# Down projection of a gated MLP on one core: products of 512 columns written as two of 256, except in the first and last block of inner rows

## The chip, the cores and the metric

The kernel runs on one core of one Trainium2 chip. The metric is the device time of one execution in microseconds; the time before is the median of three runs.

## What is computed

One layer of a hybrid decoder on 256 tokens of 1,024 features, in float32: a mixer (a matrix-memory branch and an attention branch, gated, summed, projected), a layer norm, and a gated MLP with a layer norm. The change lies in the MLP, cut here to what matters:

```python
def conv_gated_mlp(x, w_up, conv_ffn, w_down):
    u = causal_dwconv(jnp.einsum("bsd,df->bsf", x, w_up), conv_ffn)
    g, up = jnp.split(u, 2, axis=-1)
    return jnp.einsum("bsf,fd->bsd", jax.nn.silu(g) * up, w_down)

x = layer_norm(ALPHA * x + conv_gated_mlp(x, ...), ln2_g, ln2_b)
```

The inner width `D_FF` is 2,816, that is 22 blocks of 128 inner rows. The down projection multiplies 256 tokens x 2,816 inner rows by 2,816 x 1,024.

## The kernel before

**Weights as a stream.** All large weights come from HBM as steps of 128 x 2,048 floats (`load`, L80, issued on SP into three `raw` buffers). `chunk_order` (L45) writes out the order of the steps. The MLP's part of it is four `up` steps, then eight times a `dn` step followed by two `up` steps, then two more `up` steps and the last three `dn` steps. One `up` step holds one block of 128 inner rows (both halves of the gate); one `dn` step holds two blocks of inner rows with all 1,024 output columns. There are 22 `up` and 11 `dn` steps, numbered d = 0 to 10.

**Three products for one.** TensorE multiplies in a float32 form of less precision, so each operand is split into a high and a low part (`split_into`, L89: ACT writes the high part at L91, DVE the low part at L92), and `mm3` (L122) issues three products into the same accumulator: high x high at L125, then two mixed ones at L126 and L127. Each of them names a stationary operand of 128 x 128, which TensorE loads, and a moving operand, whose columns stream through.

**The up steps.** `mm_feat` (L129) takes the weights as stationary operand and the 256 tokens of `x1h`, `x1l` as moving one: 2 column blocks x 8 k-blocks x 3 = 48 products of 256 columns, into `ps_up`. ACT and DVE then apply the convolution taps and the gate (`up_evac`, L1004), and leave `hh` and `hl` (128 inner rows x 256 tokens) for a later `dn` step.

**The down steps.** `step_dn` (L1035) has the roles the other way round: `hh` or `hl` (128 tokens) is stationary, and the weight's columns move. The accumulators (`ffn` in the profile, L1038 to L1041) stay in PSUM for the whole projection. For the first 128 tokens (t = 0) they are two of 512 columns; for the second (t = 1) one of 512 and two of 256. So a block of inner rows k takes, in this order, 2 x 3 products of 512 columns for t = 0, then 3 of 512 and 2 x 3 of 256 for t = 1: nine of 512 and six of 256. Steps d = 0 to 7 (k = 0 to 15) do both halves of the tokens block by block. The last three steps (k = 16 to 21) are reordered: all six blocks for t = 0 (L1064), then all six for the 512-column accumulator of t = 1, then all six for each of its 256-column ones (L1070), so that the layer norm of the first half of the tokens (`part`, `ln_scale`, `ln2_out`) runs on DVE meanwhile.

The weight tiles `wh`, `wl` are shared by all steps; `shift` (L61) sets at which column of them a kind of step begins: 0 for the output projection `wo` and for `dn`, 16 for `up` and most of the input projection's steps, 48 or 56 for others. Accumulators named `mix` belong to `wo` steps, `ps_ga`, `ps_qb`, `ps_km`, `ps_kb`, `ps_vm` to steps of the input projection; all of these products have 256 columns. The products at L159 (`mm_early`, accumulators `ps_o`) have 512.

The instructions of each engine stand in the order in which the code issues them; there is no scheduler.

Of the kernel before, what the change touches and what calls it, by code (L numbers as in the profile page):

```python
# [24 lines left out]
NF = D_FF // P  # L25
# [44 lines left out]
class Kernel:  # L70
# [964 lines left out]
    def step_dn(self, s, d, *a):  # L1035
        if d == 0:
            self.st = [self.ln_tiles(f"2_{t}") for t in range(2)]
            a0 = [self.ps_side([P, 512], f"ffn0{h}") for h in range(2)]  # L1038
            a1 = [self.ps_side([P, 512], "ffn10"), self.ps_side([P, 256], "ffn11"), self.ps_side([P, 256], "ffn12")]
            self.acc = [list(zip(a0, ((0, 512), (512, 1024)))),  # L1040
                        list(zip(a1, ((0, 512), (512, 768), (768, 1024))))]  # L1041

        def mm(dd, kk, t, ps, cols):
            w = [x.rearrange("p (k f) -> p k f", k=2)[:, kk, slice(*cols)] for x in self.w[s - d + dd]]
            k = 2 * dd + kk
            hh, hl = (x[:, t * P:(t + 1) * P] for x in self.hid[k])
            self.mm3(ps, hh, hl, w[0], w[1], k == 0, k == NF - 1)

        def part(t, q):
            ps, cols = self.acc[t][q]  # L1050
            self.ln_part(self.st[t], self.x1[:, t, :], ps, cols)

        d0 = NF // 2 - 3
        if d < d0:
            for kk in range(2):
                for t in range(2):
                    for ps, cols in self.acc[t]:
                        mm(d, kk, t, ps, cols)
            self.w.pop(s)
            return  # L1060

        ks = [(d0 + i, kk) for i in range(3) for kk in range(2)]
        banks = self.acc[1]
        if d == d0:  # L1064
            for k in ks:
                for q in self.acc[0]:
                    mm(*k, 0, *q)
            self.evac[s] = [lambda: part(0, 0), lambda: part(0, 1), lambda: self.ln_scale(self.st[0]),
                            lambda: self.ln2_out(0)]
        else:  # L1070
            for q in banks[0:1] if d == d0 + 1 else banks[1:]:
                for k in ks:
                    mm(*k, 1, *q)
            if d == d0 + 1:
                self.evac[s] = [lambda: part(1, 0)]
# [111 lines left out]
```

## Time and profile before

| | |
|---|---|
| median of 3 runs | 497.76 us (497.49 to 497.85) |
| the profiled execution | 497.06 us |
| its span, first to last instruction | 495.3 us |
| mean granted TensorE clock | 0.995 |
| DVE, ACT busy | 370.3 us (75%), 287.9 us (58%) |
| DMA | 93.74 MB, mean 189 GB/s |

The span is 1.76 us shorter than the execution's own time; what lies around it is launch and end. In a row of the timeline stand the start in us, the duration in us, engine, line, operation, output<-inputs, the stationary and moving shape, and the count. The duration of a product (0.28 us for 256 columns) includes its way through the pipeline, and its end is modelled; products follow each other much faster than that. How fast they run is therefore read from their starts: the length of a stretch divided by the number of products that begin in it. In a row of the windows view stand the stretch (us from the span's start), its length, busy us and count of the instructions that touch it, the granted clock, the DMA engines' share and GB/s.

### The profile page before, as it was taken

What the parts mean: (1) busy time and instruction counts of PE and PEld (TensorE: products, weight loads), DVE (VectorE), ACT (ScalarE), POOL (GpSimd) and SP (SyncE); (2) the same over time, 40 slices, a digit from 0 to 9 for tenths busy, and PEclk for the clock granted to TensorE, in tenths of its full rate; (3) what the DMA queues carried; (4) which work ended last, traced back from release to release, by engine and by line L of the source; (5) the groups of instructions that cost most, each with busy time, mean ns of one, the idle gap of its engine ahead of it and who ended that gap; (6) DMA issues with size and microseconds to landing.
All of it is one profiled execution on the core that took longest, in us unless ns stands there. A gap on an engine that the chain in (4) does not pass through costs nothing.

```text
span 495.3 us, 9451 instructions
## 1 busy us (share of the span) xinstructions
PE 482.9 (97%) x3890; PEld 467.0 (94%) x3890; DVE 370.3 (75%) x659; ACT 287.9 (58%) x476; POOL 31.3 (6%) x46
## 2 busy tenths in 40 slices
PE   7999999999999999999999999999999999999992
PEld 3999999999999999999999999999999999999982
DVE  3966995788588858885677788888667766866886
ACT  4757867495648665866655524766554555554610
POOL 0600010002100110002000001000000000000001
PEclk9999999999999999999999999999999999999998
DMA  8984556456545654454945572745555456444202
GB/s 246 356 304 152 211 192 203 171 177 191 189 179 177 192 180 189 171 171 138 372 173 181 221 278 86 255 146 210 206 205 177 164 184 242 170 171 171 86 1 85
DMA packets 17884, 93.74 MB, mean 189 GB/s; under 512 B 4497, under 2 KB 4889, under 8 KB 7857
## 3 DMA queue, kind: packets, MB, share of 16 engines
q1 hardware_dynamic: 13682, 87.08, 49.4%
q0 software_dynamic: 4160, 6.07, 4.1%
q8 instruction: 30, 0.49, 0.4%
q14 instruction: 12, 0.10, 0.1%
HBM read 92.05 MB, written 2.63 MB: 191 GB/s over the span
## 4 chain that ended last, share of the span: by engine, by line
PE 96%; DMA 1%; DVE 1%; SPq 0%; ACT 0%; POOL 0%; issue 0%; POOLq 0%
PE ps_up L127 8%; PE ps_up L126 8%; PE ps_up L125 8%; PE ffn L127 4%; PE ffn L126 4%; PE ffn L125 4%; PE ps_vm L125 2%; PE ps_qm L125 2%; PE ps_vm L126 2%; PE ps_vm L127 2%; PE ps_vb L125 1%; PE ps_ga L127 1%; PE ps_ga L125 1%; PE ps_ga L126 1%; PE ps_vb L126 1%; PE ps_vb L127 1%
## 5 line engine op out<-in xcount | busy, mean ns | idle before, releaser
L92 DVE TENSOR_TENSOR wl<-raw,wh 128x1024 fp32r<-128x1024 f32 (+1 forms) x162 | 188.6, 1206 | 27.4 <-ACT wh L91 27.2
L91 ACT CAST wh<-raw 128x1024 fp32r<-128x1024 f32 (+1 forms) x162 | 158.4, 1030 | 10.7 <-DMA raw<-in_wst_dram 8.0
L127 PE MATMUL ps_up<-x1h,wl 128*128 128x256 f32 x320 | 89.9, 281 | 0.0
L126 PE MATMUL ps_up<-x1l,wh 128*128 128x256 f32 x320 | 89.9, 281 | 0.0
L125 PE MATMUL ps_up<-x1h,wh 128*128 128x256 f32 x319 | 89.7, 281 | 0.0
L126 PEld LDWEIGHTS ps_up<-x1l,wh 128*128 128x128 f32 x320 | 61.4, 192 | 0.0
L127 PEld LDWEIGHTS ps_up<-x1h,wl 128*128 128x128 f32 x320 | 60.1, 188 | 0.0
L125 PEld LDWEIGHTS ps_up<-x1h,wh 128*128 128x128 f32 x319 | 59.9, 188 | 0.0
L1020 DVE SCALAR_TENSOR_TENSOR cu<-ps_up,vec,cu 128x255 f32<-128x255 f32 (+1 forms) x80 | 33.1, 476 | 27.1 <-ACT cu L1016 26.9
L127 PE MATMUL ffn<-wh,hl 128*128 128x512 f32 (+1 forms) x110 | 38.4, 349 | 0.0
L126 PE MATMUL ffn<-wl,hh 128*128 128x512 f32 (+1 forms) x110 | 38.4, 349 | 0.0
L125 PE MATMUL ffn<-wh,hh 128*128 128x512 f32 (+1 forms) x110 | 38.3, 349 | 0.0
L91 ACT CAST hh<-cu 128x256 fp32r<-128x256 f32 x22 | 8.9, 407 | 42.9 <-DVE cu L1028 42.9
L1016 ACT ACTIVATE cu<-ps_up,vec 128x256 f32<-128x256 f32 x40 | 16.8, 472 | 28.8 <-PE ps_up L127 27.9
L126 PEld LDWEIGHTS ffn<-wl,hh 128*128 128x128 f32 x110 | 20.8, 189 | 3.0
L125 PEld LDWEIGHTS ffn<-wh,hh 128*128 128x128 f32 x110 | 20.7, 188 | 3.0
L127 PEld LDWEIGHTS ffn<-wh,hl 128*128 128x128 f32 x110 | 20.7, 188 | 2.9
L927 POOL TENSOR_TENSOR rs<-rs,mhalf 128x1 f32<-128x1 f32 x4 | 2.7, 666 | 247.6 <-DVE rs L926 247.6
L125 PE MATMUL ps_gb<-xth,wh 128*128 128x256 f32 x64 | 18.0, 282 | 0.0
L126 PE MATMUL ps_vm<-wl,xth 128*128 128x256 f32 x64 | 17.9, 280 | 0.0
L127 PE MATMUL ps_vm<-wh,xtl 128*128 128x256 f32 x64 | 17.9, 280 | 0.0
L125 PE MATMUL mix<-wh,mgh 128*128 128x256 f32 x64 | 17.8, 279 | 0.0
(295 smaller groups left out, 1442.8 us busy)
## 6 DMA issues: line engine op xcount, KB each, us to landing
raw<-in_wst_dram SPq DMA_DIRECT2D x78, 1024.0 KB, 4.9
raw<-in_wst_dram SPq DMA_DIRECT2D x5, 512.0 KB, 9.1
lnrow<-in_rows_dram POOLq DMA_DIRECT2D x4, 512.0 KB, 6.8
band<-table POOLq DMA_DIRECT2D x4, 384.0 KB, 12.3
toe<-band POOLq DMA_DIRECT2D x4, 256.0 KB, 4.4
xtok<-in_x_dram POOLq DMA_DIRECT2D x1, 1024.0 KB, 7.7
out_dram<-r SPq DMA_DIRECT2D x3, 256.0 KB, 2.0
raw<-in_wst_dram SPq DMA_DIRECT2D x2, 256.0 KB, 5.9
```

Of the source, the lines that this page charges most:

```text
L91: self.nc.scalar.copy(wh, raw)
L92: self.nc.vector.tensor_sub(wl, raw, wh.bitcast(F32))
L125: mm(ps, ah if first is None else first, bh, start=start, stop=False)
L126: mm(ps, ah, bl, start=False, stop=False)
L127: mm(ps, al, bh, start=False, stop=stop)
L927: nc.gpsimd.tensor_tensor(st["rs"], st["rs"], self.mhalf[:, 0:1], op=ALU.pow)
L1016: act.activation(cu[:, j, :], ps[:, j, :], AF.Copy, scale=tap(2, j))
L1020: v.scalar_tensor_tensor(cu[:, j, o:], ps[:, j, :S - o], tap(t, j), cu[:, j, o:], op0=ALU.mult, op1=ALU.add)
```

## The change

In `step_dn` the helper `mm` cuts a range of 512 columns into two of 256, unless the block of inner rows is the first (k = 0) or the last (k = 21). The two halves go into the two halves of the same accumulator, each with its own three products. Which parts of the operands are multiplied, and into which column of which accumulator, is unchanged; so are all other steps, all tiles and their addresses.

```diff
         def mm(dd, kk, t, ps, cols):
-            w = [x.rearrange("p (k f) -> p k f", k=2)[:, kk, slice(*cols)] for x in self.w[s - d + dd]]
             k = 2 * dd + kk
             hh, hl = (x[:, t * P:(t + 1) * P] for x in self.hid[k])
-            self.mm3(ps, hh, hl, w[0], w[1], k == 0, k == NF - 1)
+            n = cols[1] - cols[0] if k in (0, NF - 1) else 256
+            for c in range(cols[0], cols[1], n):
+                w = [x.rearrange("p (k f) -> p k f", k=2)[:, kk, c:c + n] for x in self.w[s - d + dd]]
+                o = c - cols[0]
+                self.mm3(ps[:, o:o + n], hh, hl, w[0], w[1], k == 0, k == NF - 1)
```

Here `cols` is the range of output columns of one accumulator and `ps` the accumulator. Of the 330 products of the projection before, 198 have 512 columns. 180 of them become 360 of 256; 18 stay (nine for k = 0, nine for k = 21). The program has 510 products in their place.

On PE, in the first down step (d = 0), the last product of k = 0 and the first ones of k = 1 stood like this before; `ffn_4072` and `ffn_4073` are the two accumulators of t = 0, `ffn_4076` the last of t = 1, `hh_3980` and `hl_3981` the inner rows of k = 1:

```order
L127 MATMUL ffn_4076<-wh_3878,hl_3971 128x256
L125 MATMUL ffn_4072<-wh_3878,hh_3980 128x512
L126 MATMUL ffn_4072<-wl_3879,hh_3980 128x512
L127 MATMUL ffn_4072<-wh_3878,hl_3981 128x512
L125 MATMUL ffn_4073<-wh_3878,hh_3980 128x512
```

In the changed program the same place on PE reads:

```order
L127 MATMUL ffn_4076<-wh_3878,hl_3971 128x256
L125 MATMUL ffn_4072<-wh_3878,hh_3980 128x256
L126 MATMUL ffn_4072<-wl_3879,hh_3980 128x256
L127 MATMUL ffn_4072<-wh_3878,hl_3981 128x256
L125 MATMUL ffn_4072<-wh_3878,hh_3980 128x256
L126 MATMUL ffn_4072<-wl_3879,hh_3980 128x256
L127 MATMUL ffn_4072<-wh_3878,hl_3981 128x256
L125 MATMUL ffn_4073<-wh_3878,hh_3980 128x256
```

The first three rows into `ffn_4072` are now its columns 0 to 255, the next three its columns 256 to 511. Between the 256-column products that end k = 0 and the `up` step that follows there is no product of 512 columns any more.

At the end of the projection, on PE in the changed program, the last block (k = 21, `hh_5768`) still has products of 512 columns, between pairs for t = 0 and pairs for t = 1 (`ffn_4074`):

```order
L127 MATMUL ffn_4073<-wh_5755,hl_5701 128x256
L125 MATMUL ffn_4072<-wh_5755,hh_5768 128x512
L126 MATMUL ffn_4072<-wl_5756,hh_5768 128x512
L127 MATMUL ffn_4072<-wh_5755,hl_5769 128x512
L125 MATMUL ffn_4073<-wh_5755,hh_5768 128x512
L126 MATMUL ffn_4073<-wl_5756,hh_5768 128x512
L127 MATMUL ffn_4073<-wh_5755,hl_5769 128x512
L125 MATMUL ffn_4074<-wh_5619,hh_5366 128x256
```

Of this piece only the first and last row were 512 columns wide before. DVE, ACT, POOL and SP have as many rows as before.

## The prediction

> **What bounds the kernel now.** I began with the page: TensorE (PE) is busy all the time, and the chain that ended last is almost wholly its own products, those of the up steps (`ps_up`) and of the down steps (`ffn`) ahead of all others.
>
> ```profile
> PE 482.9 (97%) x3890; PEld 467.0 (94%) x3890; DVE 370.3 (75%) x659; ACT 287.9 (58%) x476; POOL 31.3 (6%) x46
> ...
> PE 96%; DMA 1%; DVE 1%; SPq 0%; ACT 0%; POOL 0%; issue 0%; POOLq 0%
> PE ps_up L127 8%; PE ps_up L126 8%; PE ps_up L125 8%; PE ffn L127 4%; PE ffn L126 4%; PE ffn L125 4%; PE ps_vm L125 2%; PE ps_qm L125 2%; PE ps_vm L126 2%; PE ps_vm L127 2%; PE ps_vb L125 1%; PE ps_ga L127 1%; PE ps_ga L125 1%; PE ps_ga L126 1%; PE ps_vb L126 1%; PE ps_vb L127 1%
> ```
>
> The list of PE's waits has two entries, both from the first microseconds, so in the MLP nothing but PE's own pace sets the end:
>
> ```profile
> PE ps_o L159 <- ACT wh L91: 2.1, 2, 1.5
> PE warm_ps L194 <- DVE warm L191: 1.2, 1, 1.2
> ```
>
> So the question is at which pace products of 512 and of 256 columns follow each other. These rows are stretches without a break, from the windows view; the length divided by the products that begin in the stretch is the pace.
>
> ```profile
> 12.36:19.16 6.80, 6.80 (x31) 1.00 1.02 393
> ...
> 469.29:481.88 12.59, 12.59 (x54) 1.00 0.00 1
> ...
> 275.74:294.66 18.92, 18.92 (x167) 1.00 0.70 268
> ...
> 446.68:469.29 22.61, 22.61 (x192) 1.00 0.41 141
> ...
> 69.17:74.83 5.66, 5.66 (x48) 1.00 0.60 211
> 119.25:124.72 5.47, 5.46 (x48) 1.00 0.67 205
> ```
>
> First, 512 columns: the products at L159 take 6.80 / 30 = 226.7 ns (one of the 31 began earlier), those of the last down steps 12.59 / 54 = 233.1 ns. Then 256 columns: the output projection (`mix`, whose weights move as in the down steps) takes 18.92 / 167 = 113.3 ns, the last up steps 22.61 / 192 = 117.8 ns. The last two rows are the same step, `ps_ga`, in two groups of heads: 117.9 ns in the first, 114.0 ns in the second. The granted clock is 1.00 in all of them. So there are two paces for the same work, a quick one (113.3 ns per 256 columns, 226.7 per 512) and a slow one (117.8 and 233.1), and code and tile do not decide between them.
>
> What does is seen where the timeline passes from up to down steps and back (d = 0; k = 0 begins at 322.89, k = 1 at 325.67, the up steps at 328.47):
>
> ```profile
> 322.66 0.28 PE L126 MATMUL ps_up<-x1l,wh 128*128 128x256 f32 x1
> 322.78 0.28 PE L127 MATMUL ps_up<-x1h,wl 128*128 128x256 f32 x1
> 322.89 0.39 PE L125 MATMUL ffn<-wh,hh 128*128 128x512 f32 x1
> ...
> 324.99 0.28 PE L125 MATMUL ffn<-wh,hh 128*128 128x256 f32 x1
> 325.11 0.28 PE L126 MATMUL ffn<-wl,hh 128*128 128x256 f32 x1
> ...
> 325.67 0.39 PE L125 MATMUL ffn<-wh,hh 128*128 128x512 f32 x1
> 325.90 0.40 PE L126 MATMUL ffn<-wl,hh 128*128 128x512 f32 x1
> 326.14 0.39 PE L127 MATMUL ffn<-wh,hl 128*128 128x512 f32 x1
> 326.37 0.40 PE L125 MATMUL ffn<-wh,hh 128*128 128x512 f32 x1
> ...
> 327.77 0.28 PE L125 MATMUL ffn<-wh,hh 128*128 128x256 f32 x1
> ...
> 328.47 0.28 PE L125 MATMUL ps_up<-x1h,wh 128*128 128x256 f32 x1
> ...
> 339.78 0.39 PE L125 MATMUL ffn<-wh,hh 128*128 128x512 f32 x1
> ```
>
> The up steps come in slow. After the nine 512-column products of k = 0 the 256-column ones are quick (325.11 to 325.67, five steps in 0.56 us). After the nine of k = 1 they are slow again (327.77 to 328.47, six in 0.70 us: 117 ns), and the 96 products of the next two up steps stay slow: 11.31 us / 96 = 117.8 ns. So a pace is kept from product to product through a stretch of equal ones, and the 512-column products change it: nine that begin slow end quick, nine that begin quick end slow. In the timeline every down step to d = 7 repeats this.
>
> **The change part by part.** In the stretch from 325.67, where k = 1 begins, to 481.88, where the last 512-column product ends, I count the work in units of 256 columns: 18 up steps x 48 = 864; k = 1 to 15, each 9 x 2 + 6 = 24, 360; t = 0 of k = 16 to 21, 6 x 12 = 72; the 512-column accumulator of t = 1, 6 x 6 = 36. In all 1,332 units, and they took 156.21 us:
>
> ```profile
> 325.67:481.88 156.21, 156.21 (x1145) 1.00 0.47 169
> ...
> 325.67:481.88 156.21, 103.07 (x864) 1.00 0.47 169
> ```
>
> (The second row is `ps_up` alone; its 864 products confirm the count.)
>
> *Removed and added.* 180 products of 512 columns go, 360 of 256 come, 180 more weight loads with them. At the quick pace a pair takes 226.6 ns, as much as one quick product of 512 (226.7), so the extra loads cost nothing there. At the slow pace a pair takes 235.6 against 233.1, 2.5 ns more. Which applies depends on the pace when k = 1 begins. Up to 325.67 the program is unchanged, so it is quick.
>
> *What the removal changes behind it.* From 325.67 on, no 512-column product stands in the stream until k = 21. If the quick pace is kept, the up steps run at it too. I take it as kept, because equal streams keep theirs: 167 products in `mix`, and through step changes in the four steps from `ps_qb` on:
>
> ```profile
> 137.89:154.21 16.32, 16.32 (x147) 1.00 0.56 195
> 154.21:159.86 5.65, 5.65 (x50) 1.00 0.52 186
> ```
>
> The first row is `ps_qb`, `ps_km`, `ps_kb` (144 products begin in it, 113.3 ns each). The second is `ps_vm` (48 begin: 117.7 ns): there the quick pace was lost without any 512-column product. That is the evidence against me. In `ps_vm` the roles of weights and tokens swap, as they do from a down to an up step; but there the operands' start addresses change too (moving from 64 to 0 bytes past a multiple of 256, stationary from 128 to 64), while down steps, up steps and `mix` all have 64 and 128 by the program's addresses.
>
> *The sum.* 1,332 units x 113.3 ns = 150.92 us. At k = 21 the kept 512-column products leave and re-enter the quick pace: six from a quick start, then three, at 226 to 236 ns where quick ones take 226.7; that is about 9 x 5 ns = 0.05 us. 156.21 - 150.92 - 0.05 = 5.24 us saved; I say 5.2. By parts: the up steps 864 x (117.8 - 113.3) = 3.9; the pairs 180 x (233.1 - 226.6) = 1.2; the rest is 256-column products of odd k. The last 36 products (two accumulators of t = 1) stay slow: three 512-column products precede them, an odd number as with nine.
>
> *What else could hide the gain.* One round of down and two up steps lasts 16.9 us and would last 16.3. DVE, the busiest helper, has 11.72 us of work in it:
>
> ```profile
> 373.50:390.40 16.90, 16.90 (x128) 16.10 (x128) 11.72 (x18) 8.91 (x15) 0.00 (x0) 1.00 0.52 188
> ```
>
> That leaves over 4 us, and DMA is at 0.52; PE should wait for neither. At the end DVE waits for PE before its last sum:
>
> ```profile
> 486.32 0.42 DVE L919 SCALAR_TENSOR_TENSOR r<-x,ffn 128x256 f32<-128x256 f32 x1 [0.55 <-PE ffn L127]
> ```
>
> The products of t = 1 that end the stream shorten by only 15 pairs x 6.5 ns = 0.10 us, less than these 0.55, so the tail simply moves forward. The profiled execution would go from 497.06 (span 495.3) to 491.9 us; it stood 0.70 below the median, so the median goes from 497.76 to 492.5.
>
> **The rivals.** *The quick pace is lost at the first up step* (role swap, as at `ps_vm`), and nothing brings it back, since the 512-column products that did are gone. Then all is slow from 328.47 on: k = 1 takes 24 units x 113.3 ns, the rest 1,290 x 117.8 and nine 512-column products 9 x 233.1, together 156.78 us against 156.21, 0.6 us slower: 498.3. This is the case on the other side; it decides at one instruction, the first up product after k = 1. For it speaks `ps_vm`; against it, that the slow pace crosses the same border unharmed (327.77 to 339.78 above) and that `mix` follows differently addressed steps quickly. Chance 0.14. A measurement of this kernel can tell about 0.2% (1.0 us) from no change, so this would mostly show as the same: 0.10 for that, 0.04 for its exceeding 1.0 us.
>
> *Lost in every up step and found again in every down step*, because it belongs to the operands' roles after all. Then only the down steps' 468 units gain: 864 x 117.8 + 468 x 113.3 + 0.05 = 154.85 us, 1.4 saved: 496.4. For it: all up steps with these tiles are slow before. Against it: they are only ever seen behind slow products. Chance 0.05.
>
> *Each product has a cost of its own, and the paces are noise around it.* The slow rows give its size, 2.5 ns more for a pair: 180 x 2.5 = 0.45 us slower, 498.2. Against it stand the equal quick paces of one 512-column product and of a pair (226.7 and 226.6). Chance 0.03, all of it within 0.2%. By the Trainium skill (TensorE: Matmul & The Clock Gate, section Back-to-back issue gap) an isolated product costs its columns at 2.4 GHz plus about 2.5 ns, whatever its width; by that rule, which speaks against the change, 180 more products come to the same estimate, 0.45 us.
>
> **How the numbers follow.** The forecast case has 0.78 and its own range is 491.7 to 493.1: runs before spread by 0.36 us, and the quick pace may be off by 0.3 ns on 1,332 units, 0.4 us. To leave out no more than 2 in 10 the range must take in the case of 496.4 as well: 491.7 to 496.6. Faster by over 0.2%: 0.78 + 0.05 = 0.83; same 0.10 + 0.03 = 0.13; slower 0.04.
>
> **What would show it.** The windows view should give 5.44 us for a stretch of 48 `ps_up` products, not 5.65, and their mean duration should fall by the same 4 to 5 ns. The next `ffn` product after k = 1's up steps should start about 0.5 us earlier relative to 328.47. If `ps_up` stays at 117.8 and the `ffn` pairs take 235.6, the first rival is right; quick pairs beside slow up steps are the second. New waits in PE's list, or a DVE or DMA row as their releaser, would mean that the spare time was misjudged.

## The result, and the profile after

| | before | changed |
|---|---|---|
| median (4 runs each on one chip) | 497.69 us (497.49 to 497.85) | 490.5 us (490.16 to 491.2) |
| the profiled execution, and its span | 497.06, 495.3 us | 490.16, 488.4 us |
| first `ffn` product begins | 322.89 us | 321.25 us |
| first to last `ffn` product | 163.12 us | 157.92 us |
| last `ffn` product to the end of the span | 9.32 us | 9.28 us |

The changed kernel is faster: its ratio to the kernel before is 0.986, 95% interval 0.9849 to 0.9872. That is 7.2 us, 2.0 us more than the forecast and 1.2 us below its range. The last three rows of the table say where the time of the two profiled executions went: 5.20 us inside the projection, 0.04 us behind it, and 1.64 us ahead of it, where no instruction was changed. With 0.02 us less around the span they make the 6.90 us between the profiled executions. The medians lie 7.19 us apart, because before stood 0.63 us under its median in its profile and the changed kernel 0.34 us.

On the page TensorE is still the bound, with 180 more products, and its chain is the same:

```profile
PE 477.0 (98%) x4070; PEld 470.0 (96%) x4070; DVE 369.3 (76%) x659; ACT 286.2 (59%) x476; POOL 30.6 (6%) x46
...
PE 97%; DMA 1%; DVE 1%; SPq 0%; ACT 0%; issue 0%; POOL 0%; POOLq 0%
...
L127 PE MATMUL ps_up<-x1h,wl 128*128 128x256 f32 x320 | 88.5, 277 | 0.0
```

The last row is a group of up products, which the diff doesn't touch; its mean (the second number behind the bar) was 281 ns before. (The mean is of durations; the pace is read from starts, as before.) The windows view of `ps_up` in the changed kernel gives the stretch from k = 1 to the end of the last 512-column product, then the two up steps after k = 1, then the last four:

```profile
324.03:475.04 151.01, 99.22 (x864) 1.00 0.50 175
326.75:337.63 10.88, 10.88 (x96) 1.00 0.53 194
440.99:462.74 21.75, 21.75 (x192) 1.00 0.42 146
```

The stretch lasts 151.01 us where it lasted 156.21. Both groups of up steps run at 113.3 ns per product (10.88 / 96 and 21.75 / 192). In the timeline of the changed kernel one sees that the pace passes the border from down to up steps unchanged, and that the end is paced as before:

```profile
324.03 0.28 PE L125 MATMUL ffn<-wh,hh 128*128 128x256 f32 x1
...
326.64 0.28 PE L127 MATMUL ffn<-wh,hl 128*128 128x256 f32 x1
326.75 0.28 PE L125 MATMUL ps_up<-x1h,wh 128*128 128x256 f32 x1
...
343.07 0.28 PE L125 MATMUL ps_up<-x1h,wh 128*128 128x256 f32 x1
...
469.55 0.39 PE L125 MATMUL ffn<-wh,hh 128*128 128x512 f32 x1
...
470.95 0.28 PE L125 MATMUL ffn<-wh,hh 128*128 128x256 f32 x1
...
474.35 0.39 PE L125 MATMUL ffn<-wh,hh 128*128 128x512 f32 x1
...
475.05 0.28 PE L125 MATMUL ffn<-wh,hh 128*128 128x256 f32 x1
...
479.17 0.28 PE L127 MATMUL ffn<-wh,hl 128*128 128x256 f32 x1
...
479.49 0.42 DVE L919 SCALAR_TENSOR_TENSOR r<-x,ffn 128x256 f32<-128x256 f32 x1 [0.44 <-PE ffn L127]
```

The 24 products of k = 1 take 324.03 to 326.75, 113.3 ns each. One round of a down and two up steps is 326.75 to 343.07, 16.32 us. The last 36 products, behind the kept block k = 21, are slow: 35 steps from 475.05 to 479.17, 117.7 ns each.

The same rows show more than that a block of wide products (of 512 columns) turns the pace over. The nine products of k = 21 were 512 columns wide before and still are (of the piece shown ahead of the prediction for k = 21, only the first and the last row have changed their width): six for t = 0 (469.55 to 470.95), then three for t = 1 (474.35 to 475.05). Between the two groups stand 30 products of 256 columns, and they are quick (470.95 to 474.35, 113.3 ns each). So six wide products left the quick pace as it was, and three turned it over, as nine do at k = 0. All 20 profiles of this case agree: in their projections each of the 207 groups of nine wide products in a row and each of the four of three changed the pace; each of the four groups of six and of the 15 of 54 kept it. It is the odd number that counts.

The list of PE's waits in the changed kernel is as short as before, but one entry is 0.9 us smaller:

```profile
PE warm_ps L194 <- DVE warm L191: 1.2, 1, 1.2
PE ps_o L159 <- ACT wh L91: 1.2, 1, 1.2
```

This second row points to where the 1.64 us come from. Here are the first microseconds of the kernel before (the cast of the first weights on ACT, the first product that needs them, and the first of the next weight step):

```profile
6.49 0.62 ACT L91 CAST wh<-raw 128x512 fp32r<-128x512 f32 x1 [2.91 <-DMA raw<-in_wst_dram]
7.16 0.50 PE L159 MATMUL ps_o<-wh,xth 128*128 128x512 f32 x1 [1.47 <-ACT wh L91]
9.49 0.49 PE L159 MATMUL ps_o<-wh,xth 128*128 128x512 f32 x1 [0.66 <-ACT wh L91]
```

and the same three of the changed kernel:

```profile
3.98 0.62 ACT L91 CAST wh<-raw 128x512 fp32r<-128x512 f32 x1 [0.40 <-DMA raw<-in_wst_dram]
4.84 0.59 PE L159 MATMUL ps_o<-wh,xth 128*128 128x512 f32 x1
7.77 0.50 PE L159 MATMUL ps_o<-wh,xth 128*128 128x512 f32 x1 [1.19 <-ACT wh L91]
```

The first weights land 2.5 us earlier (here and below, "first weights" is the start of ACT's first cast of a weight). Some of that is spent waiting for the next step, whose first product comes 1.72 us earlier. From there PE has no further wait, and 1.64 us of it reaches the projection. The transfers are the same ones, issued on SP by the same instructions, those up to 3.11 us at the same times to 0.01 us; what differs is how fast they move. In the windows view (last column GB/s), the fifth microsecond of the kernel before:

```profile
4.00:5.00 1.00, 1.00 (x3) 0.30 (x2) 0.04 (x1) 0.00 (x0) 0.00 (x0) 1.00 0.66 92
```

and of the changed kernel:

```profile
4.00:5.00 1.00, 1.00 (x5) 0.44 (x3) 0.41 (x2) 0.60 (x1) 0.00 (x0) 1.00 0.90 251
```

The DMA view of the stretch from 2 to 6 us (packets, MB, share of the 16 engines) shows it more clearly, before and then changed:

```profile
q1 hardware_dynamic: 320, 0.54, 90.5%
```

```profile
q1 hardware_dynamic: 513, 0.99, 92.4%
```

The engines are busy in both, but a packet takes 181 ns before (90.5% of 16 x 4 us, divided by 320) and 115 ns in the changed kernel. So in the late beginning the transfers are not held back; each packet is slower.

So two theories were to be tested. On the projection: a pace is kept by history and turned over by a block of wide products (the prediction's), against "each pair of narrow products brings its own share". On the beginning: the longer program of TensorE does it, against chance between executions, buffers at other places, and the projection itself.

### The profile page after: what moved, and what is told of

The parts are those of the page before. It is cut to its first block, busy times and chain, and to the rows that moved or that the text cites. A ratio compares the mean times of both kernels' runs of the same rounds, so it can differ in the third digit from the quotient of the medians.

```text
span 488.4 us, 9811 instructions
## 1 busy us (share of the span) xinstructions
PE 477.0 (98%) x4070; PEld 470.0 (96%) x4070; DVE 369.3 (76%) x659; ACT 286.2 (59%) x476; POOL 30.6 (6%) x46
## 4 chain that ended last, share of the span: by engine, by line
PE 97%; DMA 1%; DVE 1%; SPq 0%; ACT 0%; issue 0%; POOL 0%; POOLq 0%
PE ps_up L127 8%; PE ps_up L125 8%; PE ps_up L126 8%; PE ffn L127 4%; PE ffn L126 4%; PE ffn L125 4%; PE ps_vm L125 2%; PE ps_qm L125 2%; PE ps_vm L126 2%; PE ps_vm L127 2%; PE ps_ga L125 2%; PE ps_ga L127 2%; PE ps_vb L125 2%; PE ps_vb L126 2%; PE ps_vb L127 2%; PE ps_ga L126 2%
## 5 line engine op out<-in xcount | busy, mean ns | idle before, releaser
L127 PE MATMUL ps_up<-x1h,wl 128*128 128x256 f32 x320 | 88.5, 277 | 0.0
L126 PE MATMUL ps_up<-x1l,wh 128*128 128x256 f32 x320 | 88.5, 276 | 0.0
L125 PE MATMUL ps_up<-x1h,wh 128*128 128x256 f32 x319 | 88.3, 277 | 0.0
L126 PEld LDWEIGHTS ps_up<-x1l,wh 128*128 128x128 f32 x320 | 60.2, 188 | 0.0
L127 PEld LDWEIGHTS ps_up<-x1h,wl 128*128 128x128 f32 x320 | 60.1, 188 | 0.0
L127 PE MATMUL ffn<-wh,hl 128*128 128x256 f32 (+1 forms) x170 | 47.7, 281 | 0.0
L126 PE MATMUL ffn<-wl,hh 128*128 128x256 f32 (+1 forms) x170 | 47.7, 281 | 0.0
L125 PE MATMUL ffn<-wh,hh 128*128 128x256 f32 (+1 forms) x170 | 47.7, 281 | 0.0
L126 PEld LDWEIGHTS ffn<-wl,hh 128*128 128x128 f32 x170 | 32.0, 188 | 0.3
L125 PEld LDWEIGHTS ffn<-wh,hh 128*128 128x128 f32 x170 | 31.9, 188 | 0.3
L127 PEld LDWEIGHTS ffn<-wh,hl 128*128 128x128 f32 x170 | 31.9, 188 | 0.3
L127 PE MATMUL ps_vm<-wh,xtl 128*128 128x256 f32 x64 | 17.9, 280 | 0.0
```

The source lines that it names most:

```text
L125: mm(ps, ah if first is None else first, bh, start=start, stop=False)
L126: mm(ps, ah, bl, start=False, stop=False)
L127: mm(ps, al, bh, start=False, stop=stop)
```

## The experiments on the pace

**The kernel before once more.** First, whether the early beginning is a matter of chance between two builds. No edit.

> The kernel before once more, for its first microseconds. Between the two profiles the projection part (first to last `ffn` product) went from 163.12 to 157.92 us, 5.20 shorter, and the first `ffn` product came 1.64 us earlier, in a part of the program that the change does not touch. Theory A, the beginning belongs to the built program: this run again has its first `ps_o` product after 7.1 us and its first `ffn` product at 322.9 us (within 0.2), and takes 497.7 us. Theory B, the beginning differs by chance from run to run: the first `ffn` product comes anywhere between 321 and 323 us, and the times of this program spread by 1 to 2 us. Both: 163.1 us from first to last `ffn` product.

Measured: 497.34 us, ratio 0.9991 (0.9978 to 1.0004). First weights at 6.08 us, first `ffn` product at 322.93, first to last 163.12: both are as before, so the late beginning came again with the same program.

**k = 1 wide again.** Nineteen of the twenty cut blocks stay cut.

```diff
-            n = cols[1] - cols[0] if k in (0, NF - 1) else 256
+            n = cols[1] - cols[0] if k in (0, 1, NF - 1) else 256
```

> Only k = 1 goes back to 512-column products; 19 of the 20 cut blocks stay cut. Pace theory (a stretch keeps its pace, an odd number of blocks of nine 512-column products turns it over): two wide blocks stand at the beginning now, so the pace is slow again from the first up step on, and nothing turns it until k = 21. Up steps at 117.8 ns; first to last `ffn` product 163.6 us, 0.4 longer than before, 5.6 longer than changed. Rival (the pairs themselves bring the gain, each its share): 19 of 20 shares remain, 158.2 us.

In the windows view of `ps_up`, the two up steps after k = 1:

```profile
327.69:338.98 11.29, 11.29 (x96) 1.00 0.53 189
```

That is 117.6 ns per product, and the mean of the L127 group is back at 281 ns. First to last `ffn` product: 163.57 us (expected 163.6), so nineteen cut blocks gain nothing, and lose 0.45 us. Yet the median is 496.2, ratio 0.9975 (0.9966 to 0.9984): this kernel too begins early (first `ffn` at 322.11).

**Only k = 1 cut.** One block of the twenty.

```diff
-            n = cols[1] - cols[0] if k in (0, NF - 1) else 256
+            n = cols[1] - cols[0] if k != 1 else 256
```

> Only k = 1 is cut into pairs; the other 171 wide products of k = 2 to 20 stay at 512 columns, as before. Pace theory: one wide block (k = 0) turns the pace to quick, and from then on each down step has two wide blocks, which turn it there and back, so all up steps from the fifth on run at 113.3 ns: first to last `ffn` product 159.0 us, 4.1 shorter than before, with 9 pairs instead of 180. Rival (the pairs bring the gain): 9 of 180 shares, 0.3 us, 162.8 us.

The two up steps after k = 1, in the windows view of `ps_up`:

```profile
329.15:340.03 10.88, 10.88 (x96) 1.00 0.54 194
```

All up steps from the fifth on run at 113.3 ns, and first to last is 159.05 us: nine pairs in place of nine wide products bring 4.07 of the 5.20 us. By a share for each pair it would have been 1/20. Median 493.37, ratio 0.9923 (0.9907 to 0.9939). Later wide blocks come two at a time between up steps, so they leave the pace as they found it.

**k = 1 and k = 2 wide.** Two wide blocks from k = 1 on, with two up steps between them.

```diff
-            n = cols[1] - cols[0] if k in (0, NF - 1) else 256
+            n = cols[1] - cols[0] if k in (0, 1, 2, NF - 1) else 256
```

> k = 1 and k = 2 go back to 512 columns. Pace theory: three wide blocks at the beginning, again an odd number, but the third comes one round later: the up steps of the first round (i = 4 and 5) are slow, those after k = 3 quick. First to last `ffn` product about 158.5 us, 0.6 longer than changed. Rival (the pairs bring the gain): 18 of 20 shares, 158.4 us, with all up steps at one pace. The two are told apart by the pace of `ps_up`: 117.8 in the first round and 113.3 in the others, or equal in all.

The up steps after k = 1 and those after k = 2 and 3, in the windows view of `ps_up`:

```profile
327.87:339.17 11.30, 11.30 (x96) 1.00 0.55 188
344.68:355.55 10.87, 10.87 (x96) 1.00 0.57 194
```

A wide k = 1 loses the quick pace, a wide k = 2 restores it. First to last: 158.48 us. Median 491.38, ratio 0.9877 (0.9864 to 0.9891).

**Cut up to k = 10 only.** The first wide block then is k = 11, alone in its round.

```diff
-            n = cols[1] - cols[0] if k in (0, NF - 1) else 256
+            n = cols[1] - cols[0] if k == 0 or k > 10 else 256
```

> Only k = 1 to 10 are cut into pairs. Pace theory: quick from k = 1 on through five rounds; k = 11 stands alone as a wide block in its down step and turns the pace to slow, after which each down step turns it there and back, so the up steps from then on run at 117.8 ns as before: first to last `ffn` product 160.3 us, 2.8 shorter than before. Rival (each pair brings its share): half of 5.2, 160.5 us, with the same pace of `ps_up` in the first five rounds and the others. The two are told apart by `ps_up`: 113.3 before k = 11 and 117.8 behind it. For the beginning this is 90 extra products, like the run with 90 at the end: the same place of the first `ffn` product by theory A.

The up steps before and after d = 5 (k = 10 and 11), in the windows view of `ps_up`:

```profile
394.03:404.90 10.87, 10.87 (x96) 1.00 0.54 194
410.43:421.73 11.30, 11.30 (x96) 1.00 0.51 187
```

Five rounds of quick up steps, then slow ones, and 160.28 us from first to last (expected 160.3). Median 494.55, ratio 0.9939 (0.9925 to 0.9953).

**k = 21 cut as well.** The only edit that leaves no wide product behind k = 0. The second changed line lets only the second half of an accumulator end the accumulation.

```diff
-            n = cols[1] - cols[0] if k in (0, NF - 1) else 256
+            n = cols[1] - cols[0] if k == 0 else 256
...
-                self.mm3(ps[:, o:o + n], hh, hl, w[0], w[1], k == 0, k == NF - 1)
+                self.mm3(ps[:, o:o + n], hh, hl, w[0], w[1], k == 0,
+                         k == NF - 1 and c + n == cols[1])
```

> The changed kernel, with k = 21 cut into pairs too (all but k = 0). Pace theory: no wide block stands behind k = 0, so the quick pace is never lost; the last 36 products of t = 1 run at 113.3 instead of 117.8 ns and the nine wide ones of k = 21 gain 5 ns each: first to last `ffn` product 157.7 us, 0.2 shorter than changed. Rival (slow and quick belong to the place: the last two accumulators of t = 1 are slow in all runs of the changed kernel): 157.9 us. The beginning by the length of TensorE's program: 32 packets, as changed, 490.3 us in all.

The first and the last of the last 36 products, in its timeline:

```profile
475.39 0.28 PE L125 MATMUL ffn<-wh,hh 128*128 128x256 f32 x1
...
479.36 0.28 PE L127 MATMUL ffn<-wh,hl 128*128 128x256 f32 x1
```

35 steps in 3.97 us, 113.4 ns: they are quick now. First to last is 157.71 us (expected 157.7), 0.21 less than in the changed kernel. The median is 490.37, ratio 0.9857 (0.9844 to 0.9871), the lowest of all; beside 490.5 its interval can't tell it from the changed kernel, and only the traces show the 0.21 us.

## The experiments on the beginning

The up steps, the first weights and the projection are untouched by everything below, unless a diff of `n` is shown. The packets of TensorE's instructions are a row of the page (q8: packets, MB, share); it grows with TensorE's program and not with POOL's, as the runs below show. Before has 30, the changed kernel 32, and so have `keep k = 1` and `keep k = 1, 2`, which began early; the one with a single block cut has 30 and began late. Hence the theory of the longer program.

**180 idle products behind the end.** The kernel before, with 180 small products behind the last of the program; nothing reads them.

```diff
+        idle = self.ps_main("idle")
+        for i in range(180):
+            self.nc.tensor.matmul(idle[0:32, 0, 0:32], self.x1h[:, 0, 0:32], self.x1h[:, 1, 0:32], start=True, stop=True)
```

> The kernel before, unchanged up to its last product; behind that, while TensorE is otherwise idle in the last 9 us, 180 tiny products (32 x 32) into an accumulator that nobody reads. So far the profiles with few extra products (before twice, only k = 1 cut) began their first `ffn` product at 322.9 to 323.7 us and fetched TensorE's instructions in 30 packets; those with 162 to 180 extra ones at 321.3 to 322.3 us, with 32 packets. Theory A (the beginning goes with the length of TensorE's program, whatever it does): 32 packets, first `ffn` product near 321.7 us, about 1.5 us faster than before, 496.1 us, although not one product before the end differs. Theory B (the beginning is chance, or has to do with the pairs): 322.9 us and 497.6 us. Both: 163.1 us from first to last `ffn` product.

Its page and its timeline (the first weights, then the added products):

```profile
q8 instruction: 32, 0.52, 0.4%
```

```profile
4.36 0.62 ACT L91 CAST wh<-raw 128x512 fp32r<-128x512 f32 x1 [0.78 <-DMA raw<-in_wst_dram]
...
484.77 5.85 PE L1106 MATMUL idle<-x1h 128*32 128x32 f32 x180
```

First to last stays 163.12, but the first `ffn` product comes at 321.53, and the median is 495.88 beside 497.44, ratio 0.9967 (0.9955 to 0.998). Work that nobody needs, at the other end of the program, makes it 1.6 us faster: the early beginning doesn't need the projection's pace.

**90 idle products**, otherwise the same edit.

> The same with 90 tiny products. Theory A has no number for the length between; if the beginning moves gradually with the program's length, the first `ffn` product comes at 322.3 us; if there is a step, either near 321.7 or near 323. Theory B: 322.9 us. Both: 163.1 us from first to last `ffn` product.

```profile
q8 instruction: 31, 0.51, 0.4%
```

This row is its page's. First weights at 6.39 us, first `ffn` product at 323.35, median 497.44, ratio 1.0004 (0.9993 to 1.0015): late.

**A longer program on another engine**: 360 small memsets on POOL, 20 in each of 18 up steps.

```diff
+        if i > 3:
+            idle = self.fp.tile([P, 2], F32, tag="idle", name=f"idle{i}", bufs=1)
+            for _ in range(20):
+                self.nc.gpsimd.memset(idle, 0.0)
```

> The kernel before with 360 tiny memsets on POOL, 20 in each up step from the fifth on, into a tile of their own; TensorE's program is as before. Theory A by TensorE's program alone: 30 packets, first `ffn` product at 322.9 us, 497.6 us. Theory A by the length of the whole program: first `ffn` product near 321.7 us, 496.1 us. Both: 163.1 us from first to last `ffn` product.

First weights at 6.54, median 497.51, ratio 0.9998 (0.9989 to 1.0007): late. Its page has 30 packets in q8, as before, and 14 in q14, where before has 12.

**135 and 250 idle products**, to find where it tips.

> The kernel before with 135 tiny products behind the last one. With 90 (31 packets of TensorE's instructions) the beginning was late, with 180 (32 packets) early by 1.5 us; 135 needs 32 packets. If the step lies where the 32nd packet begins: first `ffn` product near 321.7 us, 496.0 us. If the beginning goes gradually with the length: 322.3 us and 496.7 us. If it is something else that 162 and more products have in common: 323.0 us, 497.5 us.

> The same with 250 tiny products (33 packets; they take some 8 us, less than the 9 us that TensorE has left). If a program longer than the step begins early: first `ffn` product near 321.7 us, 496.0 us. If it goes by odd and even numbers of packets or another fit of the program's size: late again, 323 us and 497.5 us.

| added to before | TensorE's packets | first weights, us | median, us | ratio |
|---|---|---|---|---|
| 90 | 31 | 6.39 | 497.44 | 1.0004 (0.9993 to 1.0015) |
| 135 | 31 | 6.01 | 497.57 | 1.0001 (0.9992 to 1.001) |
| 180 | 32 | 4.36 | 495.88 | 0.9967 (0.9955 to 0.998) |
| 250 | 32 | 4.24 | 496.55 | 0.9977 (0.9968 to 0.9986) |

Both had one packet less than I had counted on, and both beginnings go with the packets they had: 31 late, 32 early. (With 250 the end itself is 9.81 us instead of 9.32, which takes back 0.5.) Up to here the beginning goes with the length of TensorE's program, and tips between 135 and 180 added products.

**A further buffer in device memory**, 32 KB, written once. If a longer program acts by moving what lies behind it, a buffer may do so too.

```diff
+        self.spare = dram.tile([P, 64], F32, name="spare")
...
+                self.nc.gpsimd.dma_start(self.spare, self.vec[:, 0:64])
```

> The kernel before with one more buffer of 32 KB in device memory, written once from POOL in the middle of the projection; TensorE's program is as before (30 packets). If the length of TensorE's program acts by shifting where the other buffers lie in memory, 32 KB more of another kind may shift them as well: first `ffn` product near 321.7 us, 496.0 us. If it acts by the program itself, or if this buffer lies elsewhere: 323.0 us, 497.5 us; this result alone does not tell those two apart.

First weights at 6.25, median 497.42, ratio 0.9991 (0.9981 to 1.0): late.

**The change's action with a short program, and with a long one.** Cut up to k = 15, which is nearly the whole change but leaves TensorE at 31 packets; then the same with 45 idle products behind the end.

```diff
-            n = cols[1] - cols[0] if k in (0, NF - 1) else 256
+            n = cols[1] - cols[0] if k == 0 or k > 15 else 256
```

> k = 1 to 15 are cut into pairs (135 more products), k = 0 and k = 16 to 21 stay wide. Pace theory: quick from k = 1 on; the 36 and 18 wide products of the last steps are even numbers of wide accumulators, so the last 36 products are quick too: first to last `ffn` product 158.1 us, 5.0 shorter than before. The beginning by the length of TensorE's program: 31 packets, so late, first `ffn` product near 323.2 us and 492.4 us in all. If instead the early beginning has to do with the pairs: first `ffn` product near 321.7 us, 490.9 us.

> The same with 45 tiny products behind the last one; nothing before them differs. Length theory: 32 packets, first `ffn` product near 321.7 us, 490.9 us in all, 1.5 less than without them. Rival: no difference, or slower by the tiny products' cost. Both: 158.1 us from first to last `ffn` product.

The first weights in the first of them:

```profile
6.50 0.62 ACT L91 CAST wh<-raw 128x512 fp32r<-128x512 f32 x1 [2.94 <-DMA raw<-in_wst_dram]
```

and in the second:

```profile
4.82 0.62 ACT L91 CAST wh<-raw 128x512 fp32r<-128x512 f32 x1 [1.21 <-DMA raw<-in_wst_dram]
```

From first to last `ffn` product both take 158.07 us. The first begins the projection at 322.87 and has a median of 492.32 us, ratio 0.9898 (0.9884 to 0.9912). The second begins it at 321.69 and has 490.84, ratio 0.987 (0.9855 to 0.9885). Here the two parts of the gain stand apart: 5.3 us for the pace, 1.5 us for the beginning.

**Longer buffers with the program before.** The weights' buffer 1 MB longer, by a step that is never read; then the small rows' buffer 64 KB longer.

```diff
-    wst = np.empty((len(order), P, 2048), np.float32)
+    wst = np.empty((len(order) + 1, P, 2048), np.float32)
+    wst[-1] = 0
```

> The kernel before with the weight stream's buffer in device memory one step (1 MB) longer; the last step is never read. If the length of TensorE's program acts by where the buffers come to lie, another length of a buffer may do so as well: first `ffn` product near 321.7 us, 496.0 us. If it acts through the program itself: 323.2 us, 497.5 us. A late beginning does not refute the placement, since nothing here shows the order of the buffers.

```diff
-    rows = np.stack([b_in[O_O:O_O + D], b_in[O_VM:O_VM + D], ln1_g, ln1_b, ln2_g, ln2_b])
+    rows = np.stack([b_in[O_O:O_O + D], b_in[O_VM:O_VM + D], ln1_g, ln1_b, ln2_g, ln2_b] + 16 * [ln2_b])
```

> The kernel before with the small `rows` buffer 64 KB longer (16 more rows that are never read); otherwise as the run with the longer weight buffer: by placement, perhaps early (321.7 us, 496.0 us); by the program itself, 323.2 us and 497.5 us.

With the longer weights' buffer, TensorE has its 30 packets and yet the first weights come early:

```profile
5.26 0.62 ACT L91 CAST wh<-raw 128x512 fp32r<-128x512 f32 x1 [1.68 <-DMA raw<-in_wst_dram]
```

Median 496.3, ratio 0.9971 (0.9959 to 0.9982). The rows' buffer does nothing: 6.42 us, 497.6, 1.0002 (0.9994 to 1.0011). So the length of the program is not the only lever; the theory as I had put it, that TensorE's program alone decides, falls.

**Both levers at once, and the rows' buffer 1 MB longer**: the changed kernel with the longer weights' buffer, to see whether the two add or cancel; and before with `256 * [ln2_b]` in place of 16.

> The changed kernel with the weight stream's buffer in device memory 1 MB longer, the last step never read. The longer buffer made the kernel before begin early with a short program (first cast of a weight at 5.26 us instead of 6.0 to 6.5). If long program and longer buffer each bring an early beginning: early here too, first `ffn` product at 321.3 to 322.3 us, 490.5 us. If both only shift the same thing and two shifts can cancel: late, 323.2 us and 492.2 us. Both: 157.9 us from first to last `ffn` product.

> The kernel before with the `rows` buffer 1 MB longer (64 KB more did nothing). If any buffer that is 1 MB longer moves the others: first cast of a weight before 5.3 us, 496.3 us. If it has to be the weight buffer itself, or one that lies ahead of it: 6.0 to 6.5 us and 497.5 us.

The first: 490.61 us, ratio 0.9862 (0.9846 to 0.9878), as the changed kernel alone. They neither add nor cancel. Its profiled execution was its longest, 493.34 us beside 490.5 to 490.79 for the others. In ACT's timeline of it, the first weights are early and the tokens' second transfer is late:

```profile
4.17 0.62 ACT L91 CAST wh<-raw 128x512 fp32r<-128x512 f32 x1 [0.59 <-DMA raw<-in_wst_dram]
7.97 0.41 ACT L91 CAST xth<-xraw 128x256 fp32r<-128x256 f32 x1 [3.18 <-DMA xraw<-in_xt_dram]
```

In the changed kernel that cast began at 6.30. Its projection took the same 157.92 us, but began at 324.43. So one and the same program can differ by some 3 us between executions, in this one ahead of the projection, and medians are needed to speak of the beginning. The second: first weights at 6.36, 497.41 us, ratio 0.9998 (0.9989 to 1.0007), late.

## Why the prediction was right in its direction, and short in size

**The pace and the sum: right.** 1,332 units at 113.3 ns and 0.05 us were to make 150.97 us, and 151.01 were measured; the up steps run at 113.3 instead of 117.8, the pairs at 113.3 each, a round lasts 16.32 us (forecast 16.3), and the last 36 products stay slow. The one weak point named, a quick pace lost when weights and tokens swap roles as in `ps_vm`, did not come about: 326.64 to 326.75 is a quick step across that border. What `ps_vm` loses it by remains unknown; the operands' addresses, which the prediction pointed to, were not tried.

**A wide block turns the pace over: right, and shown by doing.** k = 1 wide again takes the gain away with nineteen blocks still cut; k = 1 cut alone brings 4.07 of 5.20 us; k = 2 wide brings back what k = 1 wide had lost; k = 11 wide ends it in mid-course; without k = 21 the last 36 products are quick. Each of these was forecast to 0.05 us from first to last product. What counts is that nine, like three, is odd: six in a row left the pace, and so did 54 (in the kernel cut to k = 15 the products before them are quick, and the last 36 behind them begin 113.5 ns apart). The prediction had called it an odd number, and the traces bear it out. Why such products turn it over is not shown; the runs only show that they do.

**The cover: right.** PE has no new wait, and DVE's idle time before its last sum fell from 0.55 to 0.44 us where 0.10 less was expected.

**A fixed cost per product: refuted at the quick pace.** The Trainium skill (TensorE: Matmul & The Clock Gate, section Back-to-back issue gap) gives an isolated product the time of its columns at 2.4 GHz plus about 2.5 ns; by that rule 180 more products cost an estimated 0.45 us. The traces do not agree at the quick pace: a pair takes 2 x 113.3 = 226.6 ns, one wide product 226.7 (at L159; in the projection groups of wide products are slower even behind quick ones: the six of k = 21 take 1.40 us, 233 ns each). At the slow pace a pair does cost 2.5 ns more (235.6 and 233.1); with k = 1 wide, where most pairs run at that pace, the projection is 0.45 us longer than before.

**The step that failed: the sum carried over to the whole execution.** The prediction said "Up to 325.67 the program is unchanged", and its sum gave the time ahead of the projection no term: it took the 5.24 us of the stretch from the whole execution, and its range allowed only for the pace. The instructions up to there are indeed the same, but their time was not: the first weights land at 3.98 instead of 6.49 us, and the projection begins 1.64 us earlier (1.5 to 1.6 us by the medians of the runs that change only this). The row that bore on it was quoted (`ps_o` waits 2.1 us for `wh`) and was used only to say that nothing in the MLP waits. With the beginning of before, the forecast comes out to 0.2 us: the kernel cut to k = 15, whose projection is only 0.15 us longer than with the full change, has 31 packets and 492.32 us; the forecast for the full change was 492.5.

**What stays open.** Why the beginning is early. Eight programs with 32 packets of TensorE's instructions had the first weights at 3.98 to 4.82 us (one trace each); the eleven with 30 or 31 and the weights' buffer as it was, at 6.01 to 6.54. A 1 MB longer weights' buffer gives 5.26 with 30 packets. In the traces the two groups differ in how long a packet takes: between 2 and 6 us on average 181 to 191 ns in the eleven late ones, 109 to 119 ns in the nine early ones. Instruction packets at the same moment are not the reason as far as the traces record them: in all 20, only q1, the queue of the loads themselves, moves packets between 0.1 and 15 us. Where the program's parts and buffers lie in device memory could act on it, but no run shows where they lie; 32 KB, 64 KB and 1 MB added to other buffers did nothing. So it is shown that a longer program of TensorE brings the early beginning and that the projection's own action is not needed; the mechanism is not shown. Nor does the time of the first weights settle all: with 32 packets the projection began at 321.25 to 322.29 us, and once at 324.43.

## What to carry to other kernels

Read TensorE's pace from the starts of its products, stretch by stretch: busy 97% hid 4% here, and a block of a few products decided over hundreds that followed. When a gain is larger or smaller than the sum of the edit's own steps, compare first where an untouched point of the program begins in both traces. And before crediting an edit with a few tenths of a per cent, run the same program lengthened by idle work: 180 products that do nothing were worth 1.6 us.

## What the runs showed of the hardware that was not expected

- Equal products of TensorE run at one of two paces at a granted clock of 1.00: 113.3 or about 117.8 ns for 256 columns, 226.7 (at L159) or 233.1 (in the last down steps) for 512. A pace lasts through hundreds of products; three or nine products of 512 columns in a row between products of 256 turn it over, six or 54 don't.
- The load at the start depends on things outside the instructions concerned: in the fifth microsecond 92 GB/s in the kernel before, with 30 packets of TensorE's instructions, and 251 in the changed one, with 32; the first weights come between 6.01 and 6.54 us with 30 or 31 packets and between 3.98 and 4.82 us with 32. It moved the median by 1.5 to 1.6 us in the two comparisons that change nothing else (180 and 45 idle products).
- A longer buffer of which the new part is never read can do the same (5.26 us, 1.4 us of the median), while longer buffers elsewhere did not.
